# A gated layer with seven block products of half size, and the modulation's columns moved into output products

## The chip, the cores and the metric

The kernel runs on one core of a Trainium2 chip. The metric is the device time of one execution in microseconds (us). Before the change it was 2450.01 us, the median of 3 runs (2449.67 to 2454.71).

## The reference, cut to what matters

The program is three transformer-like layers for 512 tokens of width 1024, in fp32: a short-convolution mixer with a gated feed-forward layer, an SSD mixer with a gated layer, and a block with two more mixers and 32 experts. The change touches the modulation, the convolution's output and the two gated layers:

```python
mod = (silu(c) @ ada_w + ada_b).reshape(bsz, DEPTH, 2, 3, D_MODEL)   # 12 x 1024 numbers
# for each layer i, twice (mixer, gated layer):
h = rmsnorm(x, norm_g) * (1.0 + scale) + shift      # scale, shift, gate from mod
y = mixer(h)  or  swiglu_ffn(h, f_w_in[i], f_w_out[i])
x = x + gate * rmsnorm(y, norm_g2)

def swiglu_ffn(h, w_in, w_out):                     # w_in 1024 x 5632, w_out 2816 x 1024
    gate, up = split(h @ w_in, 2)
    return (silu(gate) * up) @ w_out
```

## The kernel before

Activations lie transposed: eight tiles of 128 features by 512 tokens. Every product is done in three matmuls: weights and activations are each split into a high part in a rounded type and the rest (`weight`, `split`), and high x high, rest x high and high x rest are summed (`mm`, L339 to L341). ScalarE (ACT) makes the high part (L328, L351), VectorE (DVE) or GpSimd (POOL) the rest (L329, L352). A weight tile is 128 outputs by 8 k tiles, 512 KB; it is loaded by SP's queue into a ring of four buffers (`w32`, W32 = 4) and split into a ring of five pairs (`wh`, `wl`, WHL = 5). In some phases `self.extra` names a pool with further pairs (`whx`, `wlx`, EX = 3).

A modulation column group is one row of 128 outputs of the modulation: `ada_col` (L208 to L212) loads 512 KB of `adaT` into the same ring `w32`, and one DVE instruction multiplies it with silu(c) and sums over the free axis. There are 96 of them, 24 per norm pair: 16 for scale and shift (`ada_in`), 8 for the gate (`ada_gate`), each followed by a short end step. The first 16 run in the first steps; the other 80 and the end steps stand in a list, `self.todo`, from which `self.later(n)` takes the next n. Before the change `later` is called in the convolution's loop (L508: 0, 0, 2, 5, 5, 5, 5, 4) and in the first gated layer for every gate/up pair j but the first (L655, LJ: three each), until the list is empty.

A gated layer (`ffn`) has 22 gate/up pairs in three parts (8, 7, 7). Pairs 0 to 2 (`lead` = 3) are done in token halves while the norm before is still being finished for the second half; their weights are split by GpSimd. After each part come eight output products with that part's k tiles (8, 7, 7), added into y; the last part runs in token halves, with the norm, the residual and the next norm's modulation of one half behind the products of the other (`out_and_norm`). The convolution's output products are done by `out_and_norm` too.

Where the layer is in SEVEN (only the second one, i = 1), pairs from 3 on are done by `seven`: the pair's weights (2 blocks of outputs by 2 halves of k) and h (2 halves of k by 2 halves of tokens) are multiplied as 2 x 2 blocks with seven block products in place of eight, by sums and differences of blocks. `seven_x` makes the four combined blocks of h once for the layer (t1 to t4, in the ring `tx`), `form` splits each combined weight block, and seven products of 4 k tiles by 3 matmuls by 256 tokens give gate and up. In the other layer (i = 0) a pair is two products of 24 matmuls of 512 tokens (`gu`).

The order of the instructions on each engine is made by a scheduling pass from the order in the program, the dependencies and the buffers; the norm's steps are raised in priority. The order of DMAs on SP's queue follows the program.

Of the kernel before, what the change touches and what calls it, by code (L numbers as in the profile page):

```python
# [10 lines left out]
FR = mybir.dt.float32r  # L11
# [7 lines left out]
KT = 8  # L19
# [122 lines left out]
class Kernel:  # L142
# [169 lines left out]
    def weight(self, src, k, whole=False, dst=None, eng=None, halves=None):  # L312

        nc = self.nc
        w = self.wp.tile([128, 8, 128], FT, name="w32", tag="w32", bufs=W32)
        nc.sync.dma_start(w[:, :k], src)
        if halves:
            for i, o in enumerate(halves):
                n = min(4, k - 4 * i)
                self.split([t[:, :n] for t in o], w[:, 4 * i:4 * i + n], eng)  # L320
            return [(h[:, j], l[:, j]) for h, l in halves for j in range(4)][:k]
        pool, bufs, x = self.wp, WHL, ""
        if self.extra:
            self.nw += 1
            if self.nw % (WHL + EX) >= WHL:
                pool, bufs, x = self.extra, EX, "x"
        wh, wl = dst or [pool.tile([128, 8, 128], FR, name=n, tag=n, bufs=bufs) for n in ("wh" + x, "wl" + x)]
        nc.scalar.activation(wh[:, :k], w[:, :k], AF.Copy)  # L328
        (eng or nc.vector).tensor_tensor(wl[:, :k], w[:, :k], wh[:, :k].bitcast(FT), op=OP.subtract)  # L329
        if whole:  # L330
            return wh, wl
        return [(wh[:, j], wl[:, j]) for j in range(k)]
# [164 lines left out]
    def conv_mixer(self, pp, skew, nxt):  # L497
        nc, a = self.nc, self.a
        u = []
        tiles = [m for j in range(KT) for m in (8 + j, 16 + j, j)]  # L500
        h, ahead = self.first_steps(pp, tiles[:6])
        for j in range(KT):
            cv = pp.tile([128, S + 2], FT, name="cv", tag="cv", bufs=2)
            nc.gpsimd.memset(cv[:, 0:2], 0.0)
            u.append(self.pair("hid", KT, pp))
            if j >= 2:
                ws = [self.weight(a["a_in"][m], 8) for m in tiles[3 * j:3 * j + 3]]
            self.later((0, 0, 2, 5, 5, 5, 5, 4)[j])  # L508
            product = lambda i: ahead[3 * j + i] if j < 2 else self.mtile(ws[i], h, FULL[0])
            pc = product(0)  # L510
            c = self.temp("cc")
            nc.scalar.activation(c, pc, AF.Copy)
            pv = product(1)
            nc.vector.tensor_tensor(cv[:, 2:], c, pv, op=OP.mult)
            t = self.temp("cu")
            k = lambda w: self.v("a_conv", 8 * w + j)
            nc.vector.tensor_scalar(t, cv[:, :S], k(0), None, op0=OP.mult)
            nc.vector.scalar_tensor_tensor(t, cv[:, 1:1 + S], k(1), t, op0=OP.mult, op1=OP.add)
            nc.vector.scalar_tensor_tensor(t, cv[:, 2:], k(2), t, op0=OP.mult, op1=OP.add)
            pb = product(2)  # L520
            nc.vector.tensor_tensor(t, t, pb, op=OP.mult)
            self.split(u[j], t)
        self.dump("bu", [t[0] for t in u])
        return self.out_and_norm(pp, [lambda m=m: self.weight(a["a_out"][m], 8) for m in range(KT)],
                                 u, 0, None, skew, nxt)

    def seven_x(self, pp, h, raw):

        nc = self.nc
        out = []
        for q in range(4):
            (ah, al), (bh, bl) = h[q], h[4 + q]
            a, b = raw[q], raw[4 + q]
            nc.vector.tensor_tensor(a, ah.bitcast(FT), al.bitcast(FT), op=OP.add)
            nc.vector.tensor_tensor(b, bh.bitcast(FT), bl.bitcast(FT), op=OP.add)
            b11, b12, b21, b22 = a[:, HALF[0]], a[:, HALF[1]], b[:, HALF[0]], b[:, HALF[1]]
            sub = lambda o, x, y: nc.vector.tensor_tensor(o, x, y, op=OP.subtract)
            sub(b11, b12, b11)  # L540
            sub(b12, b22, b12)
            sub(b22, b22, b11)
            sub(b21, b21, b22)
            p, r = [self.pair("tx", 8, pp) for _ in range(2)]
            self.split(p, a)
            self.split(r, b)
            at = lambda t, i: tuple(z[:, HALF[i]] for z in t)
            out.append({"b11": at(h[q], 0), "b21": at(h[4 + q], 0), "b22": at(h[4 + q], 1),
                        "t1": at(p, 0), "t3": at(p, 1), "t2": at(r, 1), "t4": at(r, 0)})
        return out  # L550

    def form(self, src):
# [65 lines left out]
    def ffn(self, pp, i, h, lead, skew, nxt):  # L618
# [4 lines left out]
        for p, js in enumerate(parts):  # L623
            hid = []
            pend = []

            def gu(j, ws, o, sl):
                n = sl.stop - sl.start
                pg = self.mtile(ws[0], h, sl)
                g = self.temp("g", n)  # L630
                nc.scalar.activation(g, pg, AF.Silu)
                pu = self.mtile(ws[1], h, sl)
                t = self.temp("gu", n)
                nc.vector.tensor_tensor(t, g, pu, op=OP.mult)
                self.split((o[0][:, sl], o[1][:, sl]), t)

            for j in js:
                o = self.pair("hid", HID, pp)
                hid.append(o)
                if j >= lead and i in SEVEN:  # L640
                    if xs is None:
                        xs = self.seven_x(pp, h, [pp.tile([128, S], FT, name="y", tag="y", bufs=8) for _ in range(KT)])
                    self.later(LJ[j])
                    g, u0, u1 = self.seven((a["f_in"][i, j], a["f_in"][i, FFT + j]), xs)
                    nc.scalar.activation(g, g, AF.Silu)
                    nc.vector.tensor_tensor(g[:, HALF[0]], g[:, HALF[0]], u0, op=OP.mult)
                    nc.vector.tensor_tensor(g[:, HALF[1]], g[:, HALF[1]], u1, op=OP.mult)
                    self.split(o, g)
                    continue
                if i in SEVEN and j == lead - 1:  # L650
                    dst = lambda: [[t.rearrange("p (k c) -> p k c", c=128) for t in self.pair("hid", HID, pp)] for _ in range(2)]
                else:
                    dst = lambda: None
                ws = [self.weight(a["f_in"][i, m], 8, halves=dst(), eng=nc.gpsimd if j < lead and 2 * j + (m != j) in FE[i] else None) for m in (j, FFT + j)]
                self.later(LJ[j])  # L655
                if p == 0 and j < lead:
                    pend.append((j, ws, o))
                    gu(j, ws, o, HALF[0])
                    if j == lead - 1:
                        for q in pend:  # L660
                            gu(*q, HALF[1])
                else:
                    gu(j, ws, o, FULL[0])

            self.fslot = None
            two = lambda: [[t.rearrange("p (k c) -> p k c", c=128) for t in self.pair("tx", 8, pp)] for _ in range(2)]
            wt = lambda m, js=js: self.weight(a["f_out"][i, m][:, js.start:js.stop], len(js),
                                              halves=two() if i in SEVEN and p == 2 and m >= WHL else None)
            if p == 2:
                return self.out_and_norm(pp, [lambda m=m: wt(m) for m in range(KT)], hid, 2 * i + 1, y, skew, nxt)  # L670
            first = y is None
            if first:
                y = [pp.tile([128, S], FT, name="y", tag="y", bufs=8) for _ in range(KT)]
            for m in range(KT):
                ps = self.mtile(wt(m), hid, FULL[0])
                if first:
                    nc.scalar.activation(y[m], ps, AF.Copy)
                else:
                    nc.vector.tensor_tensor(y[m], ps, y[m], op=OP.add)
# [1090 lines left out]
    def run(self, start=0, stop=99):  # L1770
# [4 lines left out]
        if start <= 2:  # L1775
            first = 0 if start == 0 else 2
            with ExitStack() as ada:
# [6 lines left out]
                    self.first_norm(h, *self.next_mod(first))  # L1784
                self.todo += self.ada_gate(first)
                for s in range(first + 1, 4):
                    self.todo += self.ada_in(s) + self.ada_gate(s)
                if start == 0:
                    with self.phase("conv", 2) as pp:
                        self.extra, self.nw = pp, NWC  # L1790
                        h = self.conv_mixer(pp, CS, self.next_mod(1))
                    self.dump("x00", self.x)
                    with self.phase("ffn0", TMP) as pp:
                        self.extra, self.nw = pp, NW
                        h = self.ffn(pp, 0, h, FL, FS, self.next_mod(2))
                    self.dump("x01", self.x)
                self.later(999)
# [6 lines left out]
            self.dump("x10", self.x)  # L1804
            if stop <= 3:
                return
            with self.phase("ffn1", 3) as pp:
                self.extra, self.nw = None, NW1
                h = self.ffn(pp, 1, h, FL, FS, (self.v("g_mix"), None))
            self.dump("x11", self.x)  # L1810
# [28 lines left out]

NI = 3  # L1840

SEVEN = (1,)
PD = (1, 1, 1)
RF = 1
SL = 6
# [15 lines left out]
GP = ()  # L1861
EW = 2
SQT = 4
LJ = [0] + [3] * 21
TE = (0, 1, 2)
SE = (1, 3, 5)
FE = [(0, 1, 2, 3, 4, 5)] * 2
# [53 lines left out]
```

## Time and profile before

| | before |
|---|---|
| median of 3 runs | 2450.01 us |
| profiled execution | 2448.47 us |
| its span | 2446.7 us |
| mean granted TensorE clock | 0.978 |
| busy: PE, PEld, DVE, ACT, POOL | 94%, 73%, 57%, 35%, 7% |
| loads of modulation columns | 96 of 512 KB, 4.4 us from issue to landing |
| loads of f_in weights | 88 of 512 KB, 4.1 us |
| split of a 512 KB weight | ACT 1047 ns, then DVE 1215 ns (means) |
| one modulation column on DVE | 1220 ns (median) |
| silu of c at the start | ACT 1.06 us |

PE is the matmul stream and PEld the weight loads, which lie beside it. A busy PE is not PE at its peak. An engine's idle time costs nothing unless it is the one that sets the end of a stage. In timeline rows the bracket gives the idle time before an instruction and what ended it.

### The profile page before, as it was taken

To read this page: it belongs to the slowest core of one execution; us is meant where nothing else is said; L and a number is where in the kernel's file an instruction comes from. 1 tells how busy PE (TensorE), PEld (TensorE's weight loads), DVE (VectorE), ACT (ScalarE), POOL (GpSimd) and SP (SyncE) were. 2 spreads that over 40 slices of the span, in tenths; PEclk is the share of its full clock that TensorE was granted. 3 is DMA by queue.
4 is the path that set the end of the run, shared out by engine and by line. 5 is a ranking of instruction groups with operands and counts; after the bars stand their busy time and mean duration, and the time that the engine had idled before them with its cause. 6 is when DMAs were issued, how large, how long until landed. Compare 5 with 4: busy or idle time off the path is not lost. (4 is left out here: it accounts for less than half of the span.)

```text
span 2446.7 us, 33412 instructions
## 1 busy us (share of the span) xinstructions
PE 2300.6 (94%) x12958; PEld 1786.6 (73%) x12958; DVE 1392.0 (57%) x2621; ACT 857.3 (35%) x1395; POOL 176.6 (7%) x197
## 2 busy tenths in 40 slices
PE   5998999999999999979999989999989898989798
PEld 4888888888888888879898978878876344424348
DVE  8857744646786778779495876563343222212146
ACT  3334322233765545445363535323231000000034
POOL 3003000002100000030000030020110000000001
PEclk9998999999999999989999989999998999999999
DMA  8843755641232323211332412222434999799971
GB/s 272 274 154 106 238 187 162 202 138 53 90 105 94 104 95 101 81 44 70 104 122 77 147 57 95 79 72 95 158 138 174 412 370 416 306 412 410 372 316 35
DMA packets 100530, 424.29 MB, mean 173 GB/s; under 512 B 10993, under 2 KB 13425, under 8 KB 83473
## 3 DMA queue, kind: packets, MB, share of 16 engines
q1 hardware_dynamic: 96864, 411.43, 46.6%
q0 software_dynamic: 2304, 8.39, 1.0%
q10 hardware_dynamic: 1200, 2.31, 0.3%
q8 instruction: 103, 1.69, 0.3%
q14 instruction: 59, 0.48, 0.1%
HBM read 419.92 MB, written 2.16 MB: 173 GB/s over the span
## 5 line engine op out<-in xcount | busy, mean ns | idle before, releaser
L339 PE MATMUL mm<-hh,wh 128*128 128x512 f32 (+1 forms) x1056 | 393.1, 374 | 11.2 <-ACT hh L487 10.4
L341 PE MATMUL mm<-hh,wl 128*128 128x512 f32 (+1 forms) x1056 | 394.1, 374 | 0.9 <-DVE wl L329 0.9
L340 PE MATMUL mm<-hl,wh 128*128 128x512 f32 (+1 forms) x1056 | 392.5, 372 | 1.0 <-DVE hl L409 0.7
L328 ACT ACTIVATE wh<-w 128x1024 fp32r<-128x1024 f32 (+1 forms) x211 | 220.3, 1047 | 431.1 <-PE mm L340 325.2
L329 DVE TENSOR_TENSOR wl<-w,wh 128x1024 fp32r<-128x1024 f32 (+1 forms) x192 | 232.7, 1215 | 179.2 <-ACT wh L328 175.1
L339 PEld LDWEIGHTS mm<-hh,wh 128*128 128x128 f32 x1056 | 201.6, 191 | 47.6 <-ACT hh L487 13.2
L341 PEld LDWEIGHTS mm<-hh,wl 128*128 128x128 f32 x1056 | 202.0, 191 | 35.1 <-issue 1.7
L340 PEld LDWEIGHTS mm<-hl,wh 128*128 128x128 f32 x1056 | 201.9, 191 | 35.1 <-DVE hl L409 1.3
L1547 PE MATMUL mm<-ew,xg 128*64 128x512 f32 (+2 forms) x832 | 196.0, 606 | 22.9 <-DMA ew<-w 17.2
L1547 PEld LDWEIGHTS mm<-ew,xg 128*64 128x64 f32 (+2 forms) x832 | 57.8, 130 | 135.0 <-issue 100.3
L211 DVE SCALAR_TENSOR_TENSOR w<-w,cb 128x1024 f32<-128x1024 f32 x96 | 118.9, 1242 | 55.0 <-DMA w<-adaT 54.7
L339 PE MATMUL mm<-hidh,wh 128*128 128x256 f32 (+1 forms) x415 | 140.4, 339 | 4.6 <-DVE y L437 4.6
L340 PE MATMUL mm<-hidl,wh 128*128 128x256 f32 (+1 forms) x415 | 140.3, 338 | 0.0
L341 PE MATMUL mm<-hidh,wl 128*128 128x256 f32 (+1 forms) x415 | 139.9, 338 | 0.0
L1581 PE MATMUL mm<-ew,at 128*32 128x512 f32 (+2 forms) x496 | 124.5, 599 | 10.7 <-DMA ew<-w 6.8
L1553 DVE SCALAR_TENSOR_TENSOR et<-mm,gs,eg 128x512 f32<-128x512 f32 x13 | 9.8, 751 | 168.1 <-PE mm L1547 113.2
L1653 DVE TENSOR_TENSOR x<-x,pcm 128x512 f32<-128x512 f32 (+1 forms) x112 | 65.9, 642 | 64.2 <-PE pcm L1652 64.2
L1581 PEld LDWEIGHTS mm<-ew,at 128*32 128x32 f32 (+2 forms) x496 | 31.8, 125 | 88.1 <-issue 44.3
L339 PEld LDWEIGHTS mm<-hidh,wh 128*128 128x128 f32 x415 | 80.4, 194 | 12.3 <-DVE y L437 4.8
L340 PEld LDWEIGHTS mm<-hidl,wh 128*128 128x128 f32 x415 | 80.6, 194 | 7.8
L341 PEld LDWEIGHTS mm<-hidh,wl 128*128 128x128 f32 x415 | 80.3, 194 | 7.7
L352 DVE TENSOR_TENSOR wl<-w,wh 128x512 fp32r<-128x512 f32 x114 | 74.2, 686 | 20.2 <-ACT wh L351 19.2
(554 smaller groups left out, 5131.3 us busy)
## 6 DMA issues: line engine op xcount, KB each, us to landing
ew<-w SPq DMA_DIRECT2D x106, 1024.0 KB, 13.6
ew<-w SPq DMA_DIRECT2D x120, 512.0 KB, 11.4
w<-adaT SPq DMA_DIRECT2D x96, 512.0 KB, 4.4
w<-f_in SPq DMA_DIRECT2D x88, 512.0 KB, 4.1
ewx<-w SPq DMA_DIRECT2D x26, 1024.0 KB, 12.9
w<-m_in SPq DMA_DIRECT2D x48, 512.0 KB, 3.4
w<-f_out SPq DMA_DIRECT2D x32, 448.0 KB, 3.9
w<-a_in SPq DMA_DIRECT2D x24, 512.0 KB, 4.4
```

What stands on the lines that cost most here:

```text
L211: nc.vector.scalar_tensor_tensor(w, w, 1.0, self.cb, op0=OP.mult, op1=OP.mult, accum_out=self.mod[:, j:j + 1])
L328: nc.scalar.activation(wh[:, :k], w[:, :k], AF.Copy)
L329: (eng or nc.vector).tensor_tensor(wl[:, :k], w[:, :k], wh[:, :k].bitcast(FT), op=OP.subtract)
L339: nc.tensor.matmul(out, wh, xh[:, sl], start=k == 0, stop=False)
L340: nc.tensor.matmul(out, wh, xl[:, sl], start=False, stop=False)
L341: nc.tensor.matmul(out, wl, xh[:, sl], start=False, stop=k == n - 1)
L352: (eng or self.nc.vector).tensor_tensor(l, src, h.bitcast(FT), op=OP.subtract)
L1547: nc.tensor.matmul(ps[n][rows[i]], xg[kh][:, k, s0:s0 + w0], w[i][:, k], start=kh == 0 and k == 0, stop=kh == 1 and k == 3)
L1553: nc.vector.scalar_tensor_tensor(t, ps[3], rs, g1, op0=OP.mult, op1=OP.mult)
L1581: nc.tensor.matmul(ps[rows[i]], at[:, f, rows[i]], w2(i, f), start=f == 0, stop=f == 3)
L1653: nc.vector.tensor_tensor(self.x[d][:, sl], self.x[d][:, sl], ps, op=OP.add)
```

## The change

The first gated layer is put into SEVEN, with new homes for the tiles that this needs; the modulation's columns are taken out of the gate/up pairs and put ahead of the weights of output products: one ahead of each of the convolution's eight, three ahead of each in the first part of the first gated layer, three (products 0 to 3) or two (4 to 7) in its second part. The last gate group (8 columns) moves to the second gated layer, which copies c and makes its silu again. The first layer's extra split buffers go, and the second layer gets a fourth temporary (TMP = 4 in place of 3). The right half of h's first four tiles is overwritten with t3 after the lead products, t1 gets half-size tiles of its own, and the last output weights of the layer are split into other tiles' room.

```diff
-            for i, o in enumerate(halves):
-                n = min(4, k - 4 * i)
-                self.split([t[:, :n] for t in o], w[:, 4 * i:4 * i + n], eng)
-            return [(h[:, j], l[:, j]) for h, l in halves for j in range(4)][:k]
+            out = []
+            for o in halves:
+                i, n = len(out), min(o[0].shape[1], k - len(out))
+                self.split([t[:, :n] for t in o], w[:, i:i + n], eng)
+                out += [(o[0][:, j], o[1][:, j]) for j in range(n)]
+            return out
...
-        return self.out_and_norm(pp, [lambda m=m: self.weight(a["a_out"][m], 8) for m in range(KT)],
+        def wt(m):
+            self.later(1)
+            return self.weight(a["a_out"][m], 8)
+        return self.out_and_norm(pp, [lambda m=m: wt(m) for m in range(KT)],
                                  u, 0, None, skew, nxt)
...
-            p, r = [self.pair("tx", 8, pp) for _ in range(2)]
-            self.split(p, a)
+            p = [pp.tile([128, 256], FR, name=n, tag=n, bufs=4) for n in ("t1h", "t1l")]
+            r = self.pair("tx", 4, pp)
+            self.split(p, b11)
             self.split(r, b)
...
-                        "t1": at(p, 0), "t3": at(p, 1), "t2": at(r, 1), "t4": at(r, 0)})
+                        "t1": p, "t3": at(h[q], 1), "t2": at(r, 1), "t4": at(r, 0)})
+        for q in range(4):
+            self.split(out[q]["t3"], raw[q][:, HALF[1]])
...
-                    self.later(LJ[j])
                     g, u0, u1 = self.seven((a["f_in"][i, j], a["f_in"][i, FFT + j]), xs)
...
-                self.later(LJ[j])
                 if p == 0 and j < lead:
...
-            two = lambda: [[t.rearrange("p (k c) -> p k c", c=128) for t in self.pair("tx", 8, pp)] for _ in range(2)]
-            wt = lambda m, js=js: self.weight(a["f_out"][i, m][:, js.start:js.stop], len(js),
-                                              halves=two() if i in SEVEN and p == 2 and m >= WHL else None)
+            def wt(m, js=js, p=p):
+                self.later((3, 3 if m < 4 else 2, 0)[p])
+                halves = None
+                if i in SEVEN and p == 2 and m >= WHL:
+                    halves = [self.pair("tx", 4, pp) for _ in range(2)] if m < KT - 1 else [self.pair("hid", HID, pp)] + [
+                        [pp.tile([128, 256], FR, name=n, tag=n, bufs=4) for n in ("t1h", "t1l")] for _ in range(2)]
+                    halves = [[t.rearrange("p (k c) -> p k c", c=128) for t in o] for o in halves]
+                return self.weight(a["f_out"][i, m][:, js.start:js.stop], len(js), halves=halves)
...
-                    self.todo += self.ada_in(s) + self.ada_gate(s)
+                    self.todo += self.ada_in(s) + (self.ada_gate(s) if s < 3 else [])
...
                     with self.phase("ffn0", TMP) as pp:
-                        self.extra, self.nw = pp, NW
+                        self.extra, self.nw = None, NW
...
-            with self.phase("ffn1", 3) as pp:
+            with self.phase("ffn1", TMP) as pp:
+                self.ada_start(pp)
+                self.todo += self.ada_gate(3)
                 self.extra, self.nw = None, NW1
...
-SEVEN = (1,)
+SEVEN = (0, 1)
...
-LJ = [0] + [3] * 21
```

## Rows read from the trace of the kernel before

**Rows 1.** The page: busy us (share of the span) x instructions, per engine
```profile
PE 2300.6 (94%) x12958; PEld 1786.6 (73%) x12958; DVE 1392.0 (57%) x2621; ACT 857.3 (35%) x1395; POOL 176.6 (7%) x197
```
**Rows 2.** The page: granted clock in tenths and GB/s moved, in 40 slices
```profile
PEclk9998999999999999989999989999998999999999
...
GB/s 272 274 154 106 238 187 162 202 138 53 90 105 94 104 95 101 81 44 70 104 122 77 147 57 95 79 72 95 158 138 174 412 370 416 306 412 410 372 316 35
```
**Rows 3.** Longest waits of PE (us, times, longest): 225 to 500 us; 1090 to 1400 us
```profile
PE npb L308 <- POOL nr_y L257: 2.2, 2, 1.3
...
PE mz L579 <- ACT wh L351: 1.0, 1, 1.0
```
**Rows 4.** Timeline, first gated layer: pair 3's silu, two output copies, last part's first piece
```profile
273.77 0.58 ACT L631 ACTIVATE g<-mm 128x512 f32<-128x512 f32 x1
...
337.97 0.58 ACT L677 ACTIVATE y<-mm 128x512 f32<-128x512 f32 x1
...
343.46 0.58 ACT L677 ACTIVATE y<-mm 128x512 f32<-128x512 f32 x1
...
557.88 0.42 DVE L437 TENSOR_TENSOR y<-mm,y 128x256 f32<-128x256 f32 x1 [0.59 <-PE mm L341]
```
**Rows 5.** Timeline, second gated layer, likewise; then its window 1231 to 1241
```profile
1112.77 0.28 PE L579 MATMUL mx<-hh,wh 128*128 128x256 f32 x1
...
1231.07 0.62 ACT L645 ACTIVATE g<-g 128x512 f32<-128x512 f32 x1
1241.15 0.61 ACT L645 ACTIVATE g<-g 128x512 f32<-128x512 f32 x1
...
1395.24 0.42 DVE L437 TENSOR_TENSOR y<-mm,y 128x256 f32<-128x256 f32 x1
...
1231.00:1241.00 10.00, 10.00 (x85) 10.00 (x85) 9.31 (x18) 6.59 (x15) 0.00 (x0) 1.00 0.32 107
```
**Rows 6.** Norm before the first layer: PE's stops, DVE's columns, window (PE, PEld, DVE, ...)
```profile
208.48 1.01 PE L278 MATMUL nps<-dcol,acch 128*128 128x1 f32 x4 [5.58 <-DVE acch L299]
227.45 0.58 PE L278 MATMUL nps<-dcol,accy 128*128 128x1 f32 x4 [1.78 <-DVE accy L268]
245.87 0.43 PE L308 MATMUL npb<-ident,nr_y 128*128 128x128 f32 x2 [1.26 <-POOL nr_y L257]
...
204.72 1.22 DVE L211 SCALAR_TENSOR_TENSOR w<-w,cb 128x1024 f32<-128x1024 f32 x1
223.12 1.21 DVE L211 SCALAR_TENSOR_TENSOR w<-w,cb 128x1024 f32<-128x1024 f32 x1
225.75 1.21 DVE L211 SCALAR_TENSOR_TENSOR w<-w,cb 128x1024 f32<-128x1024 f32 x1
...
226.00:236.00 10.00, 7.57 (x41) 7.30 (x42) 7.31 (x19) 1.89 (x5) 2.40 (x2) 0.66 0.56 193
```
**Rows 7.** The same stretch: two DVE additions beside a GpSimd split
```profile
195.13 2.95 DVE L420 TENSOR_TENSOR x<-x,th 128x256 f32<-128x256 f32 x2
...
195.32 2.47 POOL L329 TENSOR_TENSOR wl<-w,wh 128x1024 fp32r<-128x1024 f32 x1 [0.29 <-ACT wh L328]
```
**Rows 8.** SP's loads (first and last of seven rows); two windows, DMA share and GB/s last
```profile
254.60 3.52 SPq L210 DMA_DIRECT2D w<-adaT  x3
...
279.82 4.86 SPq L210 DMA_DIRECT2D w<-adaT  x3
...
266.00:276.00 10.00, 10.00 (x47) 8.34 (x46) 7.02 (x11) 3.62 (x5) 0.00 (x0) 1.00 0.88 305
...
1164.00:1170.00 6.00, 5.99 (x40) 5.20 (x39) 4.03 (x8) 3.86 (x5) 0.00 (x0) 1.00 0.95 337
```
**Rows 9.** Second gated layer: SP's first output loads, first output copy
```profile
1152.01 0.93 SPq L316 DMA_DIRECT2D w<-f_out  x2
1161.39 8.71 SPq L316 DMA_DIRECT2D w<-f_out  x6
...
1173.90 0.58 ACT L677 ACTIVATE y<-mm 128x512 f32<-128x512 f32 x1
```

## The prediction

> **What bounds the kernel now.** I read the busy shares first: the matrix engine (PE) is busy 94% of the span, nothing else passes 73% [rows 1]. So time is PE's matmul time plus the gaps in it, and an edit counts only if it shortens the one or moves the other. The slices place the two stages concerned: the first gated layer is slices 4 to 10 (61 us each), the second 18 to 24, and PE's granted clock is below full there only in slices 4, 18 and 24, around norms [rows 2]. Then the waits of PE. From 225 to 500 us it waits for two things only, 4.0 us in all and both before 246 us in the norm; from 1090 to 1400 us there are four kinds of waits, the longest of 1.0 us and 2.6 us together [rows 3]. In the middle of both layers PE alone sets the pace; the modulation's columns, the splits and the loads lie beside it.
>
> **Term A, seven products of half size: -7.2 us.** In the first layer a whole product (24 matmuls of 512) ends every 5.49 to 5.44 us: the output products' copies start at 337.97 and 343.46 [rows 4]. A gate/up pair is two of them, 10.88 us. The second layer already works with seven products: 84 matmuls of 256 columns, and its silus start 10.08 us apart [rows 5]. That is 0.80 us for each of 19 pairs, 15.2 us if nothing else changed. I don't take the 15.2, since the second layer also has a price for starting. Measured over the same work, from the first product of pair 3 to the first finished piece of the last output part, the first layer takes 557.88 - (273.77 - 5.44) = 289.6 us [rows 4], the second 1395.24 - 1112.77 = 282.5 us [rows 5]. The difference, 7.1 to 7.2 us, is what the edit is worth with its start and its restarts; bounds -15.2 (no start price) and -5 (the first layer starts worse). VectorE (DVE) is busy 9.31 of 10 us in such a stretch [rows 5], which is why no column may stay there: one costs 1.22 us of DVE [rows 6], and three per pair would make DVE the bound. The move of the columns is the condition of term A, and term C is its price. t3 in h's right half, t1 in small tiles and other homes for the last weights leave the work as it is: 0, bounds -0.5 and +2 (the t3 split waits for the lead products' last reads, and what is queued behind it on ScalarE are the first splits). Without the extra split buffers the ring has five; the second layer runs on five with the waits of [rows 3]: 0.
>
> **Term B, the norm's stretch without columns: -6.7 us.** Seven columns now run on DVE inside the norm between the conv's output products and the first layer's lead products. PE stops there for 5.58 us until DVE has summed x's squares; one column (204.72) stands ahead of the last sum: 1.2 us. It stops for 1.78 us until the sum of y's squares is done; three columns in a row (223.12 to 225.75) stand just before: all 1.8 us goes. Behind that stop the granted clock is 0.66 for 10 us, so some 6.8 us at 1.2 GHz, about 2 of them idle; the others would have needed half the time: 2.4 us. The stop of 1.26 us before the second half's modulation goes as well [rows 6]. Sum 1.2 + 1.8 + 2.4 + 1.3 = 6.7. Late next is the residual itself: two DVE additions took 2.95 us while GpSimd split a lead weight in 2.47 us [rows 7], and those splits stay, so 4.4 of the 5.58 us stay. Bounds: -1.2 (the order of the instructions shifts and the other stops stay) and -11.1 (all four stops go).
> The columns go to the conv's output products, one each ahead of its weight, where the weights' split buffers and not the loads are late: 0, up to +1 if a column delays a sum.
>
> **Term C, the columns in the first layer's output products: +11.9 us.** Each output product now needs four loads (three columns, one weight) through the same four load buffers, in the order of SP's queue: column, column, column, weight. What such a ring yields is seen where it was the limit: 15 loads from 254.60 to 279.82 us, 1.68 us each, with the DMA engines 88% busy; the fastest stretch at this size, 337 GB/s at 95%, is 1.55 us for 512 KB [rows 8]. I take the middle, 1.62, because the first contains waits for a split buffer and the second lasted 6 us only. First part (8 products): 4 x 1.62 = 6.48 us against 5.44 us of PE; the first weight is on time (below), so seven intervals are short by 1.04: 7.3 us. Second part (seven of eight k tiles, so 4.76 us of PE and 1.42 us for the weight): three columns need 6.28 us, three intervals x 1.52 = 4.6 us; the last four products with two columns need 4.66 us: 0. Third part: no columns, 0. Sum 11.9.
> The first weight: without columns the second layer issues two output loads at 1152.01 and the next only at 1161.39, when the last pair's buffers come free; PE's first output product starts at 1173.90 - 5.44, near 1168 [rows 9]. With columns those two slots hold columns, and column three and the weight follow at 1161.4: about 4.4 us to land and 2.3 us for the split, so 1168 (a load's time to landing and the two passes of a split, from the table). On time, no reserve; up to 2.2 us late in each part if DVE serves the columns last.
> Bounds of term C: +0.5 if loads ran at the 412 GB/s that the experts reach [rows 2] (1.27 us each), and +18.9 at 1.68 (9.0 + 5.2 + 0.3) with both first weights 2.2 us late.
> The Trainium skill (Perfetto Trace Analysis, Roofline) puts the practical single-core ceiling near 435 GB/s; by that figure a load is 1.2 us and term C is nothing (an estimate from that page). The busy shares beside the rates of [rows 8] speak against it for these loads.
>
> **Term D, eight columns in the second layer's first output products: +2.1 us.** Three products of four loads: 2 intervals x 1.04; bounds 0 and +4. The second copy of c and its silu (a load like any other and 1 us of ScalarE) lie beside the norm: 0, up to +2 if SP waits for the new tile's room with lead weights behind it. One more temporary: 0 to -1.
>
> **Term E, restarts: +1.** Now the next part's weights are loaded during output products with room to spare. Afterwards they come behind the last column; the last output product (5.44 us) covers two loads (3.2 us) and the first splits. 0 to +4.
>
> **Sum.** -7.2 - 6.7 + 11.9 + 2.1 + 1.0 = +1.1 us. The profiled execution took 2448.47 us (span 2446.7 and 1.8 around it), 1.5 below the median 2450.01. So 2449.6 against that run, 2451.1 against the median; I forecast 2450 us, no change: 0.2% is 4.9 us, about what a measurement can tell here.
>
> **Rivals.** *Faster: the supply is hidden.* If the four buffers are served at the experts' rate, C is 0.5 and D 0: -7.2 - 6.7 + 0.5 + 1 = -12.4, 2436 us; in between, 2440. For it: 412 GB/s were moved on this chip [rows 2]. Against: those are loads of up to 1 MB with many in flight, and no stretch of 512 KB loads in this ring passed 337 [rows 8]. The ceiling of the skill's page, named under term C, would make it this case. Rows alone thus put C at 9.1 or more (at 1.55 us: 7 x 0.76 + 3 x 1.25), and then a clear gain needs more of B or A as well (B's -11.1, or half the start price).
> *Slower: the load ring becomes the bound of the output products.* At 1.68 us and with the first weights late, C is 18.9 and D 4: +10, 2458 us. It decides once C and D together pass 17.8 us: from about 1.61 us per load with late first weights, 1.70 without. For it: 1.68 is the longest stretch in which this ring was the limit. If PE's stops of about 1 us per product also lowered its clock, as the stop of 1.78 us did, each such dip costs some 3 us more.
> *The seven products bring nothing*, because DVE (9.31 of 10) becomes the bound: then A is 0 and the time 2457. Against: 19 pairs of the second layer ran at 10.08 with 2.6 us of waits. It is part of the slower case.
>
> **Chances.** No change 0.37 (2445 to 2455), faster 0.34 (centre 2439), slower 0.29 (centre 2459). 2436 to 2462 leaves about a tenth on each side.
>
> **What would show it.** Right: first-layer silus 10.1 us apart; no column on DVE between conv outputs and lead products, and PE's stops there at about 4.5 us instead of 8.6; output products of the first part every 6.3 to 6.7 us, PE waiting for a weight's split behind a load, DMA share near 0.9; three stretched products in the second layer. Wrong: output products at 5.44 us (faster), or above 6.9 us, or a clock below full in them (slower); pairs above 10.5 us.

## The result, and the profile after

The changed kernel took 2471.05 us (median of 5 runs, 2464.79 to 2475.72) against 2449.67 us for the kernel before on the same chip: ratio 1.0078, 95% interval 1.0062 to 1.0093, 15 to 23 us slower. The forecast was 2450, and 2471 lies outside the range that ended at 2462. The profiled execution took 2467.54 us (span 2465.7).

The expected marks are there. In the norm's stretch (timeline of PE, kernel after; the bracket is the idle time and its releaser) the stops that [rows 6] shows behind columns are gone or small; of the longest 5.4 us stay, where 4.4 were foreseen:

```profile
209.58 1.01 PE L278 MATMUL nps<-dcol,acch 128*128 128x1 f32 x4 [5.38 <-DVE acch L299]
...
226.15 0.58 PE L278 MATMUL nps<-dcol,accy 128*128 128x1 f32 x4 [0.17 <-DVE accy L268]
227.81 0.43 PE L308 MATMUL npb<-ident,nr_y 128*128 128x128 f32 x2 [0.51 <-POOL nr_y L257]
237.60 0.58 PE L278 MATMUL nps<-dcol,acch 128*128 128x1 f32 x4 [0.37 <-DVE acch L299]
```

The silus of the last part's pairs are 10.02 and 10.08 us apart, where the prediction worked out 10.88 for the kernel before from [rows 4], and the first part's output copies, of which the first and last of eight are shown (timeline of ACT), are 6.26 us apart in the mean, where the kernel before had 5.44 (its 38.08 us in the table below, over seven intervals):

```profile
338.55 0.60 ACT L691 ACTIVATE y<-mm 128x512 f32<-128x512 f32 x1 [1.32 <-PE mm L343]
...
382.37 0.58 ACT L691 ACTIVATE y<-mm 128x512 f32<-128x512 f32 x1
...
505.08 0.62 ACT L653 ACTIVATE g<-g 128x512 f32<-128x512 f32 x1
515.10 0.62 ACT L653 ACTIVATE g<-g 128x512 f32<-128x512 f32 x1
525.18 0.62 ACT L653 ACTIVATE g<-g 128x512 f32<-128x512 f32 x1
```

What was not foreseen heads PE's longest waits from 225 to 500 us, where [rows 3] had 4.0 us in all (us in total, times, longest):

```profile
PE mm L341 <- ACT hidh L353: 6.9, 1, 6.9
PE mm L343 <- POOL hidl L354: 6.4, 1, 6.4
```

Both belong to pair 2, the last of the lead pairs, whose two weights the change splits into four `hid` tiles instead of the extra buffers. The table follows the first layer between fixed points of the two traces, in us (a "pace" is the time from the first to the last copy or addition of eight products).

| stretch | before | after | difference |
|---|---|---|---|
| start to the square sum after the convolution's output products | 191.14 | 193.03 | +1.9 |
| from there to the second half's last square sum | 52.26 | 44.57 | -7.7 |
| to pair 3's first product | 24.93 | 41.20 | **+16.3** |
| pairs 3 to 7, with the first output product | 58.76 | 59.75 | +1.0 |
| pace of part 0's output products | 38.08 | 43.82 | +5.7 |
| part 1's pairs with its first output product | 81.33 | 76.87 | -4.5 |
| pace of part 1's output products | 33.83 | 37.18 | +3.4 |
| part 2's pairs with its first piece | 77.55 | 73.60 | -4.0 |

That is +12.1 us at the last output part. The bold row ends with pair 3's first product (PE, kernel after); the kernel before had it at 273.77 - 5.44 = 268.33, by the prediction's working:

```profile
278.80 0.28 PE L588 MATMUL mx<-hh,wh 128*128 128x256 f32 x1
```

The second layer, over the stretch of term A, takes 285.4 us against 282.5. At its last norm's square sum (below; 1458.7 before) the difference is 14.2:

```profile
L278 PE MATMUL nps<-dcol,acch x56: 167/250/374, 209.6 to 1472.9; 128*128 128x1 f32 x56
```

How the 16.3 us come about is read from several engines at one moment. First come windows of the kernel after (busy us and instructions of PE, PEld, DVE, ACT, POOL; granted clock; DMA share; GB/s): PE is busy 3.05 and 2.86 of 10 us, and the clock falls to 0.77 and 0.50 of full, the latter being 1.2 GHz.

```profile
236.00:246.00 10.00, 3.05 (x23) 2.48 (x21) 8.07 (x23) 4.92 (x13) 0.71 (x1) 0.77 0.00 1
246.00:256.00 10.00, 2.86 (x11) 2.57 (x12) 6.76 (x16) 3.33 (x7) 9.20 (x3) 0.50 0.00 1
```

Then timelines of SP, ACT, POOL, PE and DVE:

```profile
199.72 4.78 SPq L316 DMA_DIRECT2D w<-f_in  x2
...
244.99 0.91 ACT L410 ACTIVATE hh<-th,mod 128x256 fp32r<-128x256 f32 x2 [1.06 <-DVE th L402]
245.80 0.40 ACT L353 ACTIVATE hidh<-gu 128x256 fp32r<-128x256 f32 x1
246.11 2.17 ACT L353 ACTIVATE hidh<-w 128x512 fp32r<-128x512 f32 x4
...
258.90 0.38 ACT L640 ACTIVATE g<-mm 128x256 f32<-128x256 f32 x1 [7.35 <-PE mm L343]
259.18 0.41 ACT L353 ACTIVATE t1h<-y 128x256 fp32r<-128x256 f32 x1
...
246.80 10.78 POOL L354 TENSOR_TENSOR hidl<-w,hidh 128x512 fp32r<-128x512 f32 x4 [7.58 <-ACT hidh L353]
...
246.78 0.58 PE L341 MATMUL mm<-hh,hidh 128*128 128x256 f32 x1 [6.95 <-ACT hidh L353]
253.94 0.58 PE L343 MATMUL mm<-hh,hidl 128*128 128x256 f32 x1 [6.36 <-POOL hidl L354]
...
259.63 0.43 DVE L354 TENSOR_TENSOR t1l<-y,t1h 128x256 fp32r<-128x256 f32 x1 [6.86 <-ACT t1h L353]
```

The loads were issued by 204.5, some 40 us ahead. The weights' copies wait in ACT's queue behind the second half's eight modulations (`hh`), which come as DVE delivers them, until 246.11. PE, in its own order, has pair 2's first half next and stands from 239.8. GpSimd then makes the four rests, and its first takes 7.08 us (below) while DVE forms the sums for the seven products; PE waits for it with its third matmul. ACT makes one copy each for t1 and t2/t4 (to 251.6) and then comes to pair 2's silu (258.90), which waits for PE; behind it stands the next copy of t1 (259.18); and DVE, which needs that copy, stands for 6.86 us. So DVE waits for ACT, ACT for PE, and PE for GpSimd.

### The profile page after: what moved, and what is told of

It is laid out like the page before. It is cut to its first block, busy times and chain, and to the rows that moved or that the text cites. A ratio compares the mean times of both kernels' runs of the same rounds, so it can differ in the third digit from the quotient of the medians.

```text
span 2465.7 us, 35246 instructions
## 1 busy us (share of the span) xinstructions
PE 2298.0 (93%) x13642; PEld 1804.7 (73%) x13642; DVE 1512.0 (61%) x2913; ACT 921.8 (37%) x1590; POOL 178.7 (7%) x199
## 5 line engine op out<-in xcount | busy, mean ns | idle before, releaser
L341 PE MATMUL mm<-hh,wh 128*128 128x512 f32 (+1 forms) x848 | 312.8, 371 | 12.8 <-ACT hh L489 10.4
L343 PE MATMUL mm<-hh,wl 128*128 128x512 f32 (+1 forms) x848 | 313.0, 370 | 0.0
L342 PE MATMUL mm<-hl,wh 128*128 128x512 f32 (+1 forms) x848 | 311.8, 368 | 1.0 <-DVE hl L411 0.7
L341 PEld LDWEIGHTS mm<-hh,wh 128*128 128x128 f32 x848 | 160.8, 190 | 41.5 <-ACT hh L489 13.2
L343 PEld LDWEIGHTS mm<-hh,wl 128*128 128x128 f32 x848 | 161.1, 190 | 26.4 <-issue 1.7
L341 PE MATMUL mm<-hidh,wh 128*128 128x512 f32 (+1 forms) x460 | 158.1, 345 | 8.4 <-DVE y L439 5.6
L343 PE MATMUL mm<-hidh,wl 128*128 128x512 f32 (+1 forms) x460 | 158.3, 345 | 4.3 <-DVE wl L331 4.3
L354 DVE TENSOR_TENSOR wl<-w,wh 128x512 fp32r<-128x512 f32 x228 | 147.6, 685 | 23.4 <-ACT wh L353 21.5
L353 ACT ACTIVATE wh<-w 128x512 fp32r<-128x512 f32 x228 | 134.1, 624 | 67.9 <-DVE w L603 32.9
L342 PE MATMUL mm<-hidl,wh 128*128 128x512 f32 (+1 forms) x460 | 158.0, 344 | 0.5 <-DVE hidl L354 0.5
L1595 PE MATMUL mm<-ew,at 128*32 128x512 f32 (+2 forms) x496 | 125.0, 611 | 12.1 <-DMA ew<-w 8.0
L211 DVE SCALAR_TENSOR_TENSOR w<-w,cb 128x1024 f32<-128x1024 f32 x96 | 116.4, 1220 | 11.9 <-DMA w<-adaT 11.3
## 6 DMA issues: line engine op xcount, KB each, us to landing
ew<-w SPq DMA_DIRECT2D x120, 512.0 KB, 11.9
```

Of the source, the lines that this page charges most:

```text
L211: nc.vector.scalar_tensor_tensor(w, w, 1.0, self.cb, op0=OP.mult, op1=OP.mult, accum_out=self.mod[:, j:j + 1])
L341: nc.tensor.matmul(out, wh, xh[:, sl], start=k == 0, stop=False)
L342: nc.tensor.matmul(out, wh, xl[:, sl], start=False, stop=False)
L343: nc.tensor.matmul(out, wl, xh[:, sl], start=False, stop=k == n - 1)
L353: self.nc.scalar.activation(h, src, AF.Copy)
L354: (eng or self.nc.vector).tensor_tensor(l, src, h.bitcast(FT), op=OP.subtract)
```

## The experiments

Theory T1: the 16.3 us are this chain, and the place of pair 2's splits in ACT's queue starts it. Rivals: T2, room or the sums for the seven products (`seven_x`) hold the layer in any case; T3, GpSimd's four rests alone; T4, the columns' loads are the loss and the stops at pair 2 would be hidden otherwise. All ratios are to the kernel before on the same chip.

**dve_splits** (in this and the later diffs `...` stands for lines and arguments left out)

```diff
-FE = [(0, 1, 2, 3, 4, 5)] * 2
+FE = [(0, 1, 2, 3), (0, 1, 2, 3, 4, 5)]
```

> Edit: in the first gated layer the residuals of pair 2's two weights are formed on VectorE instead of GpSimd; nothing else. Theory T1 (the 16.3 us lost between the second half's square sum and the first seven-product pair come from pair 2's weights being made late: their ScalarE copies stand in its queue behind the second half's modulation, at 246.1, and GpSimd then takes 2.7 us for each of four residuals): the stop of 6.95 us before the copies stays, the stop of 6.36 us behind GpSimd shrinks to 1 to 2, and the time is 2465 to 2467 against 2471. T3 (GpSimd's four residuals alone are the loss): both stops go, 2458 or less. T4 (the columns' loads explain the loss, the stops of pair 2 are hidden elsewhere): no change, 2470 to 2472.

Measured 2468.66 us, ratio 1.0070 (1.0054 to 1.0085). The stop behind GpSimd is gone, the one behind ACT is the same 6.9 us, and the stretch from the last square sum to pair 3 is 35.3 us instead of 41.2. T3 falls; 5.9 us of the 16.3 are GpSimd's part. At the layer's end (square sum at 586.3 against 588.0) only 1.7 of them are left, and the whole time lies between T1's range and T4's, its interval overlapping that of the changed kernel; so it is the stretch that decides here, not the total.

```profile
PE mm L341 <- ACT hidh L353: 6.9, 1, 6.9
```

**pair2_last**

```diff
-                    gu(j, ws, o, HALF[0])
+                    if i or j < lead - 1:
+                        gu(j, ws, o, HALF[0])
                     if j == lead - 1:
                         for q in pend:
+                            if i == 0 and q[0] == j:
+                                gu(*q, HALF[0])
                             gu(*q, HALF[1])
```

> Edit: TensorE computes pair 2's first half after the second halves of pairs 0 and 1 instead of ahead of them; the splits stay where they are. T1: four half products (4 x 2.6 us) that are ready at about 247 cover pair 2's late weights, the idle time from 239.8 to 246.8 stays, the stop of 6.36 us goes: about 6 to 7 us faster than the changed kernel, 2464 to 2465. T2 (what holds is not the weights but VectorE's and ScalarE's sums for the seven products, whose results come late in any order): TensorE reaches the first seven-product pair earlier and waits there, no gain, 2470 to 2472. T4: no change.

Measured 2458.62 us, ratio 1.0032 (1.0020 to 1.0043): 11 us of the loss are back, more than any theory said. The stretch is 26.6 us. I had counted the stops only; with PE no longer waiting for pair 2's weights, ACT's silus run on and the copy of t1 behind them, so the other links of the chain go as well. T4 falls. T2 falls as the whole cause, but not altogether: PE now stands 4.2 us in the first seven-product pair (its waits, 225 to 325 us), and pairs 3 to 7 with the first output product take 64.5 us instead of 59.8.

```profile
PE mz L588 <- ACT wh L353: 4.2, 1, 4.2
```

**early_room**

```diff
-  dst = lambda: [... self.pair("hid", HID, pp) ...]
+  dst = lambda: [... self.pair(*(("tx", 4) if i == 0 else ("hid", HID)), pp) ...]
-  ws = [self.weight(..., halves=dst(), ...) ...]
+  ws = [self.weight(..., halves=dst() if i or m != j else None, ...) ...]
-  for q in pend:
+  for q in pend[lead - 1:] + pend[:lead - 1] if i == 0 else pend:
```

> Edit: pair 2's first weight goes into the fifth slot of the weight ring and its second one into tiles that are used only later (two of the four pairs that hold the sums for the seven products), and of the second halves pair 2's comes first, so that these tiles are free again; by the order of instructions the copies now stand ahead of the second half's modulation. T1: both stops go, TensorE fills the stretch of the norm as before the change: 12 to 16 us faster than the changed kernel, 2455 to 2459. T2 (room in the tiles is not what holds, the sums for the seven products are): at most 3 us, 2468 or more. T4: no change.

Measured 2457.37 us, ratio 1.0025 (1.0013 to 1.0036). The stretch is 25.1 us against 24.9 before the change, so within this stretch all of the 16.3 is explained. In its timeline (ACT, then POOL) the copies stand at 215.89, 234.90 and 237.00, ahead of the second half's modulation:

```profile
215.89 1.06 ACT L330 ACTIVATE wh<-w 128x1024 fp32r<-128x1024 f32 x1 [1.21 <-PE mm L342]
234.90 0.62 ACT L353 ACTIVATE txh<-w 128x512 fp32r<-128x512 f32 x1
237.00 0.62 ACT L353 ACTIVATE txh<-w 128x512 fp32r<-128x512 f32 x1
240.78 1.31 ACT L410 ACTIVATE hh<-th,mod 128x256 fp32r<-128x256 f32 x3 [3.17 <-DVE th L402]
...
235.60 1.56 POOL L354 TENSOR_TENSOR txl<-w,txh 128x512 fp32r<-128x512 f32 x1 [5.72 <-ACT txh L353]
239.72 1.29 POOL L354 TENSOR_TENSOR txl<-w,txh 128x512 fp32r<-128x512 f32 x1
```

The window that had 2.86 us of PE has 10.00 at full clock:

```profile
246.00:256.00 10.00, 10.00 (x85) 10.00 (x85) 9.85 (x25) 4.88 (x13) 0.00 (x0) 1.00 0.00 1
```

Not all of it is gained for the layer. PE now begins pair 3 at 263.22 and then stands in it: its second block of weights is a sum that DVE forms at 266.24 and ACT splits at 266.96, and DVE had been busy for all of 256 to 264 us, most of it with the sums for the seven products (waits of PE, 225 to 325 us):

```profile
PE mz L588 <- ACT wh L353: 2.8, 1, 2.8
```

Pairs 3 to 7 with the first output product take 62.7 us instead of 59.8: in the changed kernel these sums and all their splits but t3's were done by 269.8, 9 us before pair 3 began. T2 is thus right for some 3 us. At the first layer's end early_room stands where the kernel before does (square sum at 576.24; 576.70 before). So seven products and a free norm gain about what the columns cost, and the next runs ask for that price.

**cols_only**

```diff
-SEVEN = (0, 1)
+SEVEN = (1,)
-                        self.extra, self.nw = None, NW
+                        self.extra, self.nw = pp, NW
```

> Edit: the columns are where the change puts them, but the first gated layer has ordinary pairs throughout, with the three extra split buffers, as before the change. By the terms of the prediction (norm stretch -6.7, columns in output products +11.9, second layer's 8 columns +2.1): +7.3, 2457. By what the two traces show of these terms (-7.7, +9.6, +2.9 and +1.9 in the convolution's output product): +6.7, 2456.5. If the columns carry the loss (T4), it is as slow as the changed kernel, 2470 or more.

Measured 2469.98 us, ratio 1.0075 (1.0061 to 1.0089): +18, not +7. T4 gave the number, but not for its reason: output products ran at 5.44 us from the second interval on. With the extra buffers the output weights are split during pairs 4 to 7, and ACT's queue stands again, this time for their loads among 24 columns (timeline of ACT):

```profile
331.18 1.06 ACT L330 ACTIVATE whx<-w 128x1024 fp32r<-128x1024 f32 x1 [6.72 <-DMA w<-f_out]
```

Behind it is the last pair's `hidh`, and PE waits for that (waits of PE, 250 to 500 us; then the window around it):

```profile
PE mm L341 <- ACT hidh L353: 5.6, 1, 5.6
```

```profile
326.00:336.00 10.00, 3.85 (x11) 2.45 (x10) 6.61 (x10) 2.59 (x4) 0.00 (x0) 0.67 0.87 307
```

Theory S: an output product with four loads waits for transfers, and that is the columns' price. Rival V: DVE's 1.3 us for each column is.

**bare_cols**

```diff
-        nc.sync.dma_start(w, self.a["adaT"][j])
+        if not self.bare:                     # bare: only in the first layer's output products
+            nc.sync.dma_start(w, self.a["adaT"][j])
-        nc.vector.scalar_tensor_tensor(w, w, 1.0, self.cb, ...
+        nc.vector.scalar_tensor_tensor(w, self.cb if self.bare else w, 1.0, self.cb, ...
```

> Edit, on top of early_room: the 44 columns of the first layer's output products keep their VectorE operation and their slot of the load ring, but nothing is loaded for them (their sums are of other data). S: the transfers are the whole price, the output products run at TensorE's pace (5.44 and 4.76 us): 9 to 13 us faster than early_room, 2445 to 2448. V: the price is in VectorE's queue, 2455 to 2458.

Only its first layer is read: later stages work on other values, and the whole time, 2642.47 us, is no measure (from the last square sum ahead of the experts to the first behind them it took 757 us instead of 561 to 571). Part 0's pace is 38.5 us against 44.9 in early_room, with PE never idle (window below), part 1's 34.2 against 36.3; the layer ends 6.8 us earlier. S holds for the output products; I had expected 9 to 13.

```profile
327.00:366.00 39.00, 39.00 (x178) 32.17 (x177) 31.49 (x50) 14.85 (x21) 0.00 (x0) 1.00 0.46 149
```

**even_cols**

```diff
-                self.later((3, 3 if m < 4 else 2, 0)[p])
+                self.later((2, 2, 2 if m < 6 else 0)[p])
```

> Edit, on top of early_room: the first layer's 44 columns stand 2 ahead of each output product of parts 0 and 1 and 2 ahead of the first six of part 2, instead of 3 (part 0) and 3 or 2 (part 1). Theory S (supply: a product that needs four 512 KB loads waits for them, 44.9 us for seven products of part 0 against 38.1 without columns; three loads fit): part 0 goes back to 5.4 to 5.6 us a product and part 1 to 4.8, which gives back 8 to 11 us; part 2 pays 0 to 3: 2447 to 2452. Rival V (VectorE's 1.3 us for each column, and not the loads, holds the products: the work is only moved): 2456 to 2459.

Measured 2457.44 us, ratio 1.0019 (1.0004 to 1.0033): no gain beyond what the intervals allow. Part 0 runs at 38.1 us, as without columns, part 1 at 34.4, and the last part begins 7.0 us earlier (551.22). But its 12 columns take 7.1 us there: PE waits 4.0 us for splits of weights, the granted clock is 0.86 from 552 to 577 us, and the layer ends at 576.30. S is right about the pace and wrong about the sum; the time is in V's range, but not for V's reason, since parts 0 and 1 did speed up.

**weight_first**

```diff
-                self.later((3, 3 if m < 4 else 2, 0)[p])
-                return self.weight(...)
+                w = self.weight(...)
+                self.later((3, 3 if m < 4 else 2, 0)[p])
+                return w
```

> Edit, on top of early_room: in each output product of both layers the weight's load is issued ahead of its columns and not behind them. S: the same bytes in the same ring of four, so the pace of 6.4 us stays; the first product of a part gains its three columns' time once, 1.5 to 2 us for each of two parts: 2453 to 2456. A rival (what a product waits for is the place of its load behind the columns): the price of the columns goes nearly whole, 2446 to 2449.

Measured 2453.06 us, ratio 0.9994 (0.9982 to 1.0006), the best with seven products in both layers, and as good as the kernel before. The time is S's, the pace is not: part 0's is 40.2 us where S kept 44.9, part 1's 36.6. The loads run at the same 311 GB/s in both kernels (327 to 366 us), and the pairs between the parts pay 1.7 us more, so a part of the price is moved and not saved. The trace's layer end (576.61) doesn't show the gain that the medians do. Of this, 1.8 us lie ahead of the edit: the convolution's square sum stands at 194.51 against 192.68, with the granted clock at 0.91 from 160 to 180 us. The rest I don't put to a place.

**seven_alone**

```diff
+LJ = [0] + [3] * 21
...
+                    self.later(LJ[j])         # ahead of each pair, as before the change
-            self.later(1)                     # none in a_out, none in f_out, none in the second layer
-                self.later((3, 3 if m < 4 else 2, 0)[p])
```

> Edit, on top of early_room: all columns where they stood before the change (three in each pair of the first layer, none in output products, none in the convolution's output product, none in the second layer). With cols_only this makes the four corners of two factors. By busy time: VectorE is busy 47.0 of 50 us in the seven-product pairs of early_room, 9.5 of 10.1 a pair, and three columns add 3.9: 13.3 a pair against 10.9 before the change, about 18 pairs: +43, with the columns' price of the output products gone (-12): 2485 to 2495. If VectorE's busy time hides slack (a rival): the columns fit, 2440 to 2446.

Measured 2486.68 us, ratio 1.0133 (1.0112 to 1.0154), within the range. Silus are 12.05 us apart (mean of six intervals from 396.36 to 468.68), where I had expected 13.3.

**in_pairs**

```diff
+                    self.later(1 if i == 0 and j in range(9, 21) else 0)     # in the pair
-                self.later((3, 3 if m < 4 else 2, 0)[p])                     # and behind the weight:
+                self.later((2, 2, 0)[p] if i == 0 else (1, 1 if m == 0 else 0, 0)[p])
```

> Edit, on top of early_room: weights' loads ahead of columns in output products, two columns for each product of the first layer's parts 0 and 1, and the other 12 one in each of the pairs 9 to 20 (even_cols had them in part 2, where they took 7.1 us); the second layer's 8 columns one to a product. Theory V2 (VectorE is the bound of a seven-product pair: busy 9.4 of 10.1 us, so a column of 1.3 adds 0.6 to 0.7): 12 columns cost 7 to 8 us and the time is that of even_cols less 1 to 3 for the order of loads: 2450 to 2455 against 2452 for the kernel before. Rival (a pair has slack enough, what counts is only how many bytes an output product loads): 8 to 10 us under early_room, 2445 to 2448.

Measured 2456.74 us, ratio 1.0018 (1.0007 to 1.0030). The last part begins at 557.46, 6.2 us later than in even_cols, the layer ends at 574.98. Part 1's pairs with columns take 10.65 us (silus 372.97 to 415.55, four intervals) where early_room's took 10.07. The rival falls; V2 has the price, about 0.6 us a column, though the time lies above its range.

**spread**

```diff
-            self.later((0, 0, 2, 5, 5, 5, 5, 4)[j])
+            self.later((0, 0, 5, 6, 6, 6, 6, 5)[j])
-                    self.later(1 if i == 0 and j in range(9, 21) else 0)     # the rest as in_pairs,
+                    self.later(1 if i == 0 and j in (15, 17, 19, 20) else 0) # and a_out's columns behind its weights
```

> Edit, on top of early_room: as in_pairs, but eight of the 12 columns are not in pairs: the convolution takes 34 columns instead of 26 in its input products (each of these loads three weights in 16.3 us of TensorE's time), its output product one each behind the weight, and four pairs (15, 17, 19, 20) one each. S: the input products have room for one more load each and pay 0 to 2 us, the four columns in pairs 0 to 3, and parts 0 to 2 run at TensorE's pace: 6 to 9 us under early_room, 2445 to 2449, and under the kernel before. Rival (VectorE is full in the input products too, 1.3 us a column): 8 to 10 us there, no gain, 2454 to 2458.

Measured 2459.30 us, ratio 1.0027 (1.0015 to 1.0039): no gain, as the rival had it, and a little above its range. The convolution's eight columns more cost 7 us at one place (PE below, kernel spread; 1.42 in the changed kernel): the last split of the convolution comes late on ACT. It waits there for DVE's last product of the convolution (173.68), and ahead of that stands a column (172.53) that had itself waited 0.63 us for its load; whether VectorE's work or the loads set this place was not separated.

```profile
175.07 0.79 PE L341 MATMUL mm<-hidh,wh 128*128 128x256 f32 x2 [6.43 <-ACT hidh L353]
```

**norm_free**

```diff
-LJ = [0] + [3] * 21
+LJ = [0] * 5 + [4] * 17
```

> Edit, on the kernel before the change: LJ, the number of columns ahead of each pair of the first layer, is 0 for pairs 0 to 4 and 4 from pair 5 on instead of 3 from pair 1 on; ordinary pairs throughout, nothing else. It takes the columns out of the norm's stretch (VectorE) and leaves them under ordinary pairs, in which VectorE was busy 7.0 to 8.3 of 10 us with up to 302 GB/s loaded and TensorE never stopped. Theory C (the norm's stretch gains 7 to 8 us whatever else is done, and a column costs nothing only where TensorE's own 10.9 us of a pair outlast VectorE and the loads): 5 to 8 us faster than before, 2443 to 2446. Rival (four columns a pair are over what a pair hides, 0.6 us each as in output products): the gain goes again, 2449 to 2453.

Measured 2449.88 us, ratio 0.9985 (0.9973 to 0.9997), 1 to 7 us under the kernel before on its chip (2453.37), and the lowest ratio of all, though its interval overlaps that of weight_first. In the middle, 3.5 us, it is less than theory C's 5 to 8 and more than nothing, so the rival has a part. The norm's stretch gives 4.6 us (190.94 to 238.62: 47.7 against 52.3); 1.9 come back up to the first output copy (324.18), and the layer ends 2.5 to 2.9 us earlier. Four columns a pair cost little, not nothing.

**before_again**

> The kernel before the change once more, for a second profile. In the first one the stretch from the last square sum ahead of the experts (1821.3) to the first of the gated norm (2382.3) took 561.0 us; in ten kernels that share its instructions it took 565.8 to 570.8. Theory R (the experts' loads vary from run to run): here again anywhere in 560 to 571, and no part of the changed kernel's loss is to be put there. Rival (something in the changed first part, though the order of instructions is the same, slows the experts): 561 again, and 4 to 9 us of the loss lie there.

Measured 2456.91 us in one run, profiled (rows: last square sum ahead of the experts, first one behind them). The experts' stretch took 566.4 us: the spread is of runs, and R holds. The first layer ends at 576.31, 0.4 us from the first profile, so for the kernel before differences up to there are good to some tenths. With a column ahead of each of the convolution's output weights two profiles agree less well: nine kernels with the same convolution have its square sum between 191.7 and 194.5 us.

```profile
L278 PE MATMUL nps<-dcol,accy x112: 164/250/373, 11.8 to 1824.5; 128*128 128x1 f32 x112
...
L278 PE MATMUL nps<-dcol,ewx x24: 164/250/353, 2390.9 to 2446.4; 128*128 128x1 f32 x24
```

## Why the prediction was wrong, by its own steps

- **Term A** failed in one step: "Without the extra split buffers the ring has five; the second layer runs on five with the waits of [rows 3]: 0". Without these buffers pair 2's weights are split into `hid` tiles, and that cost +16.3. The clause beside it, on the other new homes, argues in the same way: it prices the amount of work, which is the same, and not its place in ACT's queue, though it names the queue for t3's splits. The second layer was a false witness: there the same tiles are split without such a chain. early_room took back 16.1 us of this stretch by the place of these splits and the order of the halves. The part that was worked out looks right, but in part by luck: -7.2 foreseen (and +1 for restarts, E), and the three stretches with pairs gave +1.0, -4.5 and -4.0, together -7.4. In early_room, where the chain is gone, they gave +4.0, -4.3 and -3.5, together -3.8, because the sums for the seven products now hold the first such pair. That is outside the bound of -5.
- **Term B**: -6.7 foreseen, -7.7 in the norm and +1.9 in the convolution's output products, where up to +1 was allowed: PE waited there for the last split (1.42 and 0.45 us), which is nearly all of it, in a place that spreads by 2.8 us between kernels with this convolution. Together -5.8. One reading was wrong: the column at 204.72 was not worth 1.2 us of the first stop, of which 5.38 of 5.58 us stay.
- **Term C**: +11.9 foreseen, +9.1 measured (5.7 of 7.3, 3.4 of 4.6). The loads came a little faster than 1.62 us each: 6.26 us for four in part 0, 1.57 each. bare_cols shows that they set the pace, and weight_first that their order moves part of the price. But the price depends on what the other edits leave: with ordinary pairs (cols_only) it was a stop of 5.6 us ahead of the outputs.
- **Term D**: +2.1 foreseen, +2.4 to +2.9 against the two profiles of before (285.4 us against 283.0 and 282.5).
- **Sum**: with -7.4, -5.8, +9.1 and +2.9 the forecast of no change would have stood (-1.2 against +1.1); the 16.3 decides, though without it some 4 us come back elsewhere, most of them in term A: early_room begins its last output part at 558.24, 0.4 us behind the kernel before. The trace thus has some 14 of the 15 to 23 us; the rest is not located, and the experts alone spread over 10 us between executions. For the same reason early_room's +3 to +9 us at an unchanged first layer are explained only in part, by 3.4 to 4.4 us more between the layer's end and the second layer's last square sum (886.4 against 882.0 and 883.0).
- **The rivals**: "load ring becomes the bound" was true of the output products, at a smaller price than its +10. None had a wait at the lead pairs.
- **The condition of A**, that no column may stay in a seven-product pair, is shown: seven_alone, +33. Two factors, four corners: columns moved alone +18, seven products alone +33, both +6 (with the splits in time), neither 0. The edits need each other; neither is worth anything alone, and together they lose 3 to 9 us (early_room) or come out level (weight_first).

## What to carry to other kernels

When a tile gets a new home, look up which instructions stand ahead of its writer in the queue of the in-order engine, and who needs what stands behind it; the work being the same says nothing. And background work (here 512 KB and 1.3 us of DVE for each column) is free only under a stage whose bound has room beside it: the ordinary pairs carried four columns nearly for nothing, the seven-product pairs, the output products and the convolution each asked about 0.6 to 0.9 us for one more. A faster stage that uses up its slack sends the bill for what it used to hide; moving only the columns that stood in the norm's stretch (norm_free) was the better change.

## What the runs showed of the hardware

One row of the kernel after (duration min/median/max in ns) shows GpSimd's rests of pair 2 in both layers: the same instruction took 1.38 us in the median and 7.08 at most.

```profile
L354 POOL TENSOR_TENSOR hidl<-w,hidh x8: 1267/1375/7082, 246.8 to 1104.5; 128x512 fp32r<-128x512 f32 x8
```

The longest is the first, from 246.80 to 253.9. DVE ran without a pause from 246.7 to 252.8 then, and most of that were sums and differences of two SBUF tiles; once it stood, the other three took 3.7 us together. In early_room, with smaller DVE operations beside them, two rests took 1.56 and 1.29. The Trainium skill (SBUF — State Buffer, Who interferes with whom) says that a DVE instruction with two SBUF inputs contends with a GpSimd instruction that reads SBUF; the trace agrees, by about 5.7 us here. dve_splits, where DVE makes pair 2's rests, gained about that (5.9 us in this stretch).

A stop of PE also costs clock: 0.50 in 246 to 256 us, with 2.86 us of PE in the window, and still 0.88 in 256 to 266 us, where PE was busy throughout.
